# Later modulations by 64 rows and both column halves: a diffusion-transformer layer on one NeuronCore

## The chip, the cores and the metric

The kernel runs on one core of a Trainium2 chip. The metric is the device time of one execution in microseconds (us), the median over several runs. Lower is better. All arithmetic is float32; matrix products are made of float32 operands split into a high and a low part (`fp32r`), with three matmuls for each product.

## The reference, cut to what matters

The layer has nine modulation vectors for the latent tokens (from `c`) and nine for the context tokens (from `c_ctx`). Each is a row vector of 1024 times a 1024x1024 block of `w_mod`, plus a bias:

```
mod_lat = silu(c) @ w_mod[layer] + b_mod[layer]        # 9 * 1024 columns
mod_ctx = silu(c_ctx) @ w_mod[layer] + b_mod[layer]
ml = split(mod_lat, 9);  mc = split(mod_ctx, 9)
x  = x  + 0.5 * ml[2] * swiglu(modulate(rms_norm(x),  ml[0], ml[1]), ffn1_w_in, ffn1_w_out)
cx = cx + 0.5 * mc[2] * swiglu(modulate(rms_norm(cx), mc[0], mc[1]), ffn1_w_in, ffn1_w_out)
# mixers (convolution and attention) of x and cx, modulated by m = 3, 4, gated by ml[5]
# second feed-forward of x, modulated by m = 6, 7, gated by ml[8]; final norm
```

There are 1024 latent tokens, 256 context tokens, 1024 channels, 8 query heads and 2 key heads of 128, and feed-forward layers of 2816.

## The kernel before

The program is one long sequence of stages: start-up (tokens are loaded and transposed, the first modulations made), the first feed-forward's inner products (22 iterations `j`, each of which is a Winograd-like set of products `self.product(i)` of 12 matmuls of 128x128 weights by 512 columns), its outer products, the mixers' inner products, the heads (`tokens2`), attention, the merge, and the second feed-forward. Work off the main line is written as Python generators, whose steps are run between pieces of the main line. A scheduler then orders every engine's queue; matmuls marked `pinned` keep their place in the program. Each engine runs its own queue in order. Loads and stores are issued by SP's queue, in order.

The weights of each product pass through three buffers: `raw` (loaded), a high part made by ScalarE (`act.copy`, a cast) and a low part made by VectorE (`tensor_sub`), both named `wl` or `wh` with four buffers each. VectorE also adds the products' results up from PSUM (`u`, `v`, `b`, `c`), from five banks of tag `s`. So VectorE works both ahead of the TensorE (the low parts) and behind it (the additions).

The later modulations are such side work. `later_mod(m, ...)` (line 272) makes modulation `m`, one half of 512 columns after the other. For each half it loads eight tiles `rawm` of 128 rows by 512 columns (with `by_four`, four tiles that hold two of them), multiplies each by a column of `silu_c` and adds it to an accumulator `macc` on VectorE (one accumulator for each stream, latent and context), with a `yield` after each tile. After four steps more (`WAIT`) the accumulator is split into `acch` and `accl`, after six more steps two matmuls with a column of ones (`ones_r`) sum it over the partitions into one row of PSUM (bank tag `t`), ScalarE copies the row out in another order (`mrow`), SP's queue moves it into columns (`mcol`), and VectorE adds the bias into `modl` or `modc`. A half has 8 + 4 + 6 + 1 = 19 steps, a modulation 38.

What runs the steps: in the first feed-forward `STEPS` gives the number of steps after each iteration `j` (0, then 7, 7, 7, then 6 each, 0 at 13, 11 each from 14 on), with two steps after each of 14 context blocks behind iteration 13 (the batch). These steps are, in this order, the context's half of m = 1, the context's m = 0, the context's norm (`normc`), and m = 2, 3, 4 for both streams. m = 5 runs 8 steps at a time in the mixers, m = 6 and 7 (`by_four`) 8 at a time in the heads, and m = 8 three at a time in the second feed-forward.

```
STEPS = (0, 7, 7, 7, 6, 6, 6, 6, 6, 6, 6, 6, 6, 0, 11)
BATCH = 2
WAIT = 4
tpool = ctx.enter_context(tc.tile_pool(name="tpool", bufs=11))      # ttile: rawm, macc, acch, accl, mrow and others
```

Of the kernel before, what the change touches and what calls it, by code (L numbers as in the profile page):

```python
# [18 lines left out]
P = 128  # L19
D = 1024  # L20
KD = D // P
# [22 lines left out]
WAIT = 4  # L44
# [7 lines left out]
def tile_dit_layer(  # L52
# [73 lines left out]
    def ps_t(n=512):  # L126
        return psum.tile([P, 512], F32, tag="t", name=uniq("pt"), bufs=2)[:, :n]
# [62 lines left out]
    silu_c = const.tile([P, 16], F32, name="silu_c")  # L190
    act.activation(out=silu_c[:], in_=cols[:, :16], func=AF.Silu)

    modl = const.tile([P, 72], F32, name="modl")
    modc = const.tile([P, 40], F32, name="modc")


    def split(src, hi, lo, lo_eng=None, hi_eng=None):

        if hi_eng is dve:
            dve.tensor_copy(out=hi, in_=src)  # L200
        else:
            act.copy(out=hi, in_=src)
        (lo_eng or dve).tensor_sub(out=lo, in0=src, in1=hi.bitcast(F32))
# [65 lines left out]
            transpose(pr[:, j * P : (j + 1) * P], y[:, j : j + 1].to_broadcast([P, P]), pinned=True)  # L269
        return pr  # L270

    def later_mod(m, halves=(0, 1), streams=None, by_four=False):

        if streams is None:
            streams = (0, 1) if m < 5 else (0,)
        for half in halves:
            raws = fetch_mod(m, half, False) if by_four else None
            accs = [ttile(f"macc{v}") for v in streams]
            o = m * D + half * 512
            for k in range(KD):  # L280
                if by_four:
                    raw = raws[k // 2][:, k % 2]
                else:
                    raw = ttile("rawm")
                    load(out=raw, in_=w_mod[0, k * P : (k + 1) * P, o : o + 512])
                for acc, v in zip(accs, streams):
                    s = silu_c[:, v * 8 + k : v * 8 + k + 1]
                    if k == 0:
                        dve.tensor_scalar(out=acc, in0=raw, scalar1=s, scalar2=None, op0=ALU.mult)
                    else:  # L290
                        dve.scalar_tensor_tensor(out=acc, in0=raw, scalar=s, in1=acc, op0=ALU.mult, op1=ALU.add)
                yield
            for _ in range(WAIT):
                yield
            parts = []
            for acc in accs:
                ah, al = ttile("acch", dt=F32R), ttile("accl", dt=F32R)
                split(acc, ah, al)
                parts.append((ah, al))
            for _ in range(6):  # L300
                yield
            for (ah, al), v in zip(parts, streams):
                mod, pm = (modl, modc)[v], ps_t()
                matmul(pm[:1], ones_r[:], ah, start=True, stop=False, pinned=True)
                matmul(pm[:1], ones_r[:], al, start=False, stop=True, pinned=True)
                row = ttile("mrow")
                act.copy(
                    out=row[:1].rearrange("o (p j) -> o j p", j=4), in_=pm[:1].rearrange("o (j p) -> o j p", j=4)
                )
                mcol = small("mcol", 4)  # L310
                sp.dma_start(out=mcol[:], in_=row[:1])
                c0 = m * 8 + half * 4
                dve.tensor_add(out=mod[:, c0 : c0 + 4], in0=mcol[:], in1=bcol[:, c0 : c0 + 4])
            yield

    def fetch_mod(m, half, pinned=True):
        raws = []
        for kk in range(KD // 2):
            raw = atile("rawm", (P, 2, 512))
            o = m * D + half * 512  # L320
            load(raw[:], w_mod[0, kk * 256 : (kk + 1) * 256, o : o + 512].rearrange("(a p) n -> p a n", p=P), pinned)
            raws.append(raw)
        return raws
# [833 lines left out]
    hc = Context("h1ch", F32R), Context("h1cl", F32R)  # L1157
    normc = modulated_norm(xc, *hc, CC, gain1, mods, 0)

    def all_later_mods():  # L1160
        yield from later_mod(1, (1,), (1,))
        yield from later_mod(0, (0, 1), (1,))
        part_gain(gain1["c"], 0, "g1", "c", 0, 8)
        for _ in normc:
            yield
        for m in range(2, 5):
            yield from later_mod(m)
# [744 lines left out]
```

## Time and profile before

| | |
|---|---|
| runs | median 2631.92 us of 3 (2631.13 to 2632.04) |
| span of the profiled execution, first to last instruction | 2631.1 us (the runs' median is 0.8 us above it) |
| TensorE matmuls | busy 2609.9 us, 12665 instructions |
| TensorE weight loads | busy 2176.1 us |
| VectorE | busy 1997.4 us, 3360 instructions |
| ScalarE | busy 1183.5 us |
| GpSimd | busy 545.8 us |
| DMA | 384.69 MB, mean 146 GB/s |
| granted TensorE clock, mean | 0.998 |

"Busy" is the union of an engine's instructions; a matmul's record spans its passage through the pipeline, so consecutive matmuls overlap in the records. In the rows below, L90 is a helper through which every operation passes, so groups are told apart by the names of what they write and read. `x180` is a count. A tile's buffer number is left out in the profile (`ps` for every bank of that name).

### The profile page before, as it was taken

How to read it: one execution, taken by the hardware profiler on the slowest of the kernel's cores; microseconds unless marked ns; L12 is line 12 of the kernel's file. 1: busy time of each engine (PE TensorE's matmuls, PEld its weight loads, DVE VectorE, ACT ScalarE, POOL GpSimd, SP SyncE). 2: the span in 40 equal slices, each digit the busy share in tenths (PEclk: the TensorE clock that was granted, in tenths of full speed). 3: DMA queues.
4: the chain of work that ended last, by engine and by line, in shares of the span. 5: the costliest groups of instructions: out<-in, count | busy, mean ns of one | idle time of the engine just before them, and what ended most of it. 6: DMA issues, size and time to landing. Idle time of an engine off the chain costs nothing.

```text
span 2631.1 us, 35379 instructions
## 1 busy us (share of the span) xinstructions
PE 2609.9 (99%) x12665; PEld 2176.1 (83%) x12665; DVE 1997.4 (76%) x3360; ACT 1183.5 (45%) x2343; POOL 545.8 (21%) x425
## 2 busy tenths in 40 slices
PE   8999999999999999999999999999999999999998
PEld 5888899888888888888888888888888888888888
DVE  5888976877897879977788576676457886667996
ACT  6533454333454642333355566574237333334553
POOL 0133201221010034333022112132000442321100
PEclk9999999999999999999999999999999999999999
DMA  8665465345973365542522322113425653227831
GB/s 324 205 210 182 149 215 173 106 131 185 327 184 117 124 205 160 163 134 89 200 77 85 86 87 65 33 37 118 158 85 176 201 167 96 90 80 286 191 84 65
DMA packets 372905, 384.69 MB, mean 146 GB/s; under 512 B 19686, under 2 KB 256376, under 8 KB 372728
## 3 DMA queue, kind: packets, MB, share of 16 engines
q1 hardware_dynamic: 363288, 363.52, 42.1%
q0 software_dynamic: 9440, 18.91, 4.3%
q8 instruction: 99, 1.62, 0.2%
q14 instruction: 78, 0.64, 0.1%
HBM read 310.45 MB, written 71.86 MB: 145 GB/s over the span
## 4 chain that ended last, share of the span: by engine, by line
PE 94%; DVE 3%; DMA 1%; ACT 1%; issue 1%; SPq 0%; DVEq 0%; ACTq 0%
PE ps L90 81%; PE pt L90 8%; PE po L90 6%; DMA rawm<-in_w_mod_dram 1%; DVE xb L90 0%; DVE wl L90 0%; DVE macc L90 0%; DVE m L90 0%; DVE y L90 0%; DVE pts L90 0%; DMA xtok<-in_x_dram 0%; DVE x L90 0%; DVE r L90 0%; SPq L90 0%; DVE rs_t L90 0%
## 5 line engine op out<-in xcount | busy, mean ns | idle before, releaser
L90 PE MATMUL ps<-r,wl 128*128 128x512 f32 x5196 | 1198.3, 390 | 3.6 <-ACT r L90 1.3
L90 PEld LDWEIGHTS ps<-r,wl 128*128 128x128 f32 x5196 | 972.4, 188 | 207.7 <-ACT r L90 1.6
L90 ACT CAST wl<-sum 128x512 fp32r<-128x512 f32 x218 | 134.1, 622 | 294.4 <-PE ps L90 227.1
L90 ACT CAST wl<-raw 128x512 fp32r<-128x512 f32 x287 | 178.2, 622 | 193.1 <-PE ps L90 147.9
L90 DVE TENSOR_TENSOR wl<-raw,wl 128x512 fp32r<-128x512 f32 x287 | 210.2, 736 | 61.0 <-ACT wl L90 59.3
L90 DVE TENSOR_TENSOR wl<-sum,wl 128x512 fp32r<-128x512 f32 x218 | 196.9, 904 | 33.5 <-ACT wl L90 32.3
L90 POOL TENSOR_TENSOR sum<-raw 128x512 f32<-128x512 f32 x55 | 76.4, 1389 | 680.6 <-DMA raw<-in_ffn_w_in_dram 345.3
L90 DVE SCALAR_TENSOR_TENSOR macc<-rawm,silu_c,macc 128x512 f32<-128x512 f32 x178 | 145.4, 835 | 17.1 <-DMA rawm<-in_w_mod_dram 16.6
L90 DVE TENSOR_TENSOR u<-u,ps 128x512 f32<-128x512 f32 x186 | 126.5, 680 | 32.2 <-PE ps L90 32.1
L90 ACT CAST rh<-hid 128x512 fp32r<-128x512 f32 x132 | 82.2, 623 | 139.4 <-PE ps L90 112.3
L90 POOL TENSOR_TENSOR sum<-raw,sum 128x512 f32<-128x512 f32 x55 | 76.7, 1395 | 287.0 <-DVE wl L90 284.0
L90 DVE TENSOR_TENSOR pts<-pt,pts 128x512 fp32r<-128x512 f32 x160 | 107.3, 686 | 36.2 <-ACT pts L90 34.6
L90 DVE TENSOR_REDUCE m<-ps 128x1 f32<-128x256 f32 (+1 forms) x192 | 111.0, 597 | 29.4 <-PE ps L90 28.5
L90 ACT CAST pts<-pt 128x512 fp32r<-128x512 f32 x160 | 92.2, 597 | 85.5 <-PE pt L90 84.4
L90 PE MATMUL ps<-rh,wl 128*128 128x512 f32 x360 | 122.8, 390 | 0.0
L90 PE MATMUL ps<-wh,r 128*128 128x512 f32 x384 | 120.7, 392 | 0.0
L90 DVE TENSOR_TENSOR rl<-hid,rh 128x512 fp32r<-128x512 f32 x132 | 91.0, 693 | 29.9 <-ACT rh L90 19.4
L90 ACT CAST wh<-raw 128x512 fp32r<-128x512 f32 (+1 forms) x85 | 68.2, 803 | 95.5 <-PE ps L90 74.9
L90 PE MATMUL ps<-kl,qs 128*128 128x512 f32 x384 | 104.0, 394 | 0.1
L90 PE MATMUL ps<-rh,wh 128*128 128x512 f32 x300 | 102.8, 389 | 0.0
L90 PE MATMUL ps<-y,wc 128*128 128x512 f32 x384 | 95.3, 391 | 0.2 <-DVE g L90 0.2
L90 POOL TENSOR_TENSOR sum<-sum,raw 128x512 f32<-128x512 f32 x55 | 87.8, 1597 | 5.7 <-PE ps L90 3.9
(325 smaller groups left out, 5102.3 us busy)
## 6 DMA issues: line engine op xcount, KB each, us to landing
raw<-in_ffn_w_in_dram SPq DMA_DIRECT2D x131, 512.0 KB
raw<-in_ffn_w_out_dram SPq DMA_DIRECT2D x72, 512.0 KB
raw<-in_w_in_dram SPq DMA_DIRECT2D x64, 512.0 KB
rawm<-in_w_mod_dram SPq DMA_DIRECT2D x104, 256.0 KB
hid<-hd SPq DMA_DIRECT2D x40, 512.0 KB
ucd<-uc SPq DMA_DIRECT2D x33, 512.0 KB
rawm<-in_w_mod_dram SPq DMA_DIRECT2D x32, 512.0 KB
ws<-in_ffn_w_out_dram POOLq DMA_DIRECT2D x26, 512.0 KB, 6.4
```

Source lines behind the costliest of these rows:

```text
L90: inst = getattr(self.engine, name)(*args, **kw)
```

## The change

Each step now takes 64 rows of `w_mod` and all 1024 columns: the tile `rawm` holds columns 0 to 511 of the 64 rows in partitions 0 to 63, and columns 512 to 1023 of the same rows in partitions 64 to 127. One accumulator thus holds both halves. Two DMAs fill a tile, one for each half of the partitions. A step multiplies by a column of `silu_r`, which has the 64 values of `silu` in both halves of the partitions; four small DMAs make it from `silu_c` once (`spread_silu`). At the end one pair of matmuls with two one-hot columns (`halves_r`: ones in partitions 0 to 63, and in 64 to 127) sums the two halves into two rows of PSUM, one copy takes both out, two DMAs turn them into eight columns, and one addition adds the bias. A modulation has 16 + 4 + 6 + 1 = 27 steps. The context's half of m = 1 keeps the old form, under the name `later_half`.

```diff
+    one_hot = const.tile([P, 2], F32, name="one_hot")
+    pool.memset(one_hot[:], 0.0)
+    for h in range(2):
+        pool.memset(one_hot[h * 64 : (h + 1) * 64, h : h + 1], 1.0)
+    halves_r = const.tile([P, 2], F32R, name="halves_r")
+    act.copy(out=halves_r[:], in_=one_hot[:])
+    silu_r = const.tile([P, 32], F32, name="silu_r")
+
+    def spread_silu():
+        by = silu_r[:].rearrange("p (a s) -> p a s", s=2)
+        for h in range(2):
+            for i in range(2):
+                sp.dma_start(out=by[h * 64 : (h + 1) * 64, :, i], in_=silu_c[i * 64 : (i + 1) * 64, :])
...
-    def later_mod(m, halves=(0, 1), streams=None, by_four=False):
+    def later_mod(m, streams=None, by_four=False):
...
+        def rows(t, n):
+            return w_mod[0, t * 64 : (t + n) * 64, m * D : (m + 1) * D].rearrange("(a r) (h n) -> h r a n", r=64, h=2)
+        accs = [ttile(f"macc{v}") for v in streams]
+        for t in range(16):
+            if by_four and t % 8 == 0:
+                raws = []
+                for i in range(4):
+                    raw = atile("rawm", (P, 2, 512))
+                    for h in range(2):
+                        load(raw[h * 64 : (h + 1) * 64], rows(t + 2 * i, 2)[h])
+                    raws.append(raw)
+            if by_four:
+                raw = raws[t % 8 // 2][:, t % 2]
+            else:
+                raw = ttile("rawm")
+                for h in range(2):
+                    load(raw[h * 64 : (h + 1) * 64], rows(t, 1)[h, :, 0])
+            for acc, v in zip(accs, streams):
+                s = silu_r[:, v * 16 + t : v * 16 + t + 1]
...
+            yield
+        yield from mod_sums(accs, streams, m * 8, halves_r, 2)
...
+    def mod_sums(accs, streams, c0, sums, n):
+        for _ in range(WAIT):
+            yield
...
+        for (ah, al), v in zip(parts, streams):
+            mod, pm = (modl, modc)[v], ps_t()
+            matmul(pm[:n], sums[:], ah, start=True, stop=False, pinned=True)
+            matmul(pm[:n], sums[:], al, start=False, stop=True, pinned=True)
+            row = ttile("mrow")
+            act.copy(
+                out=row[:n].rearrange("o (p j) -> o j p", j=4), in_=pm[:n].rearrange("o (j p) -> o j p", j=4)
+            )
+            mcol = small("mcol", 8)
+            for h in range(n):
+                sp.dma_start(out=mcol[:, h * 4 : (h + 1) * 4], in_=row[h : h + 1])
+            dve.tensor_add(out=mod[:, c0 : c0 + 4 * n], in0=mcol[:, : 4 * n], in1=bcol[:, c0 : c0 + 4 * n])
+        yield
...
+    spread_silu()
     def all_later_mods():
-        yield from later_mod(1, (1,), (1,))
-        yield from later_mod(0, (0, 1), (1,))
+        yield from later_half(1, 1, (1,))
+        yield from later_mod(0, (1,))
```

The built programs show how this moves instructions. On the TensorE, behind iteration 6 of the first feed-forward (counted from 0), the program before has the sum of the first half of m = 0 (`pt` is the PSUM row, `ps` the products, `r` their moving operand, `wl` the low part of their weights):

```order
L90 MATMUL ps_2062<-r_155_777,wl_1995 128x512 x3
L90 MATMUL ps_2062<-r_178_875,wl_1995 128x512 x3
L90 MATMUL ps_2062<-r_205_993,wl_1995 128x512 x3
L90 MATMUL ps_2062<-r_224_1068,wl_1995 128x512 x3
L90 MATMUL pt_2079<-acch_1967,ones_r 1x512
L90 MATMUL pt_2079<-accl_1968,ones_r 1x512
L90 MATMUL ps_2100<-r_162_802,wl_2021 128x512 x3
L90 MATMUL ps_2100<-r_185_900,wl_2021 128x512 x3
L90 MATMUL ps_2100<-r_212_1018,wl_2021 128x512 x3
L90 MATMUL ps_2100<-r_227_1079,wl_2021 128x512 x3
```

The sum of the second half stands 62 rows further on, again as one pair with `ones_r`. The changed program has no sum at the first place, and one pair for both halves behind iteration 8, 11 rows ahead of where the second half's stood:

```order
L90 MATMUL ps_2329<-r_155_784,wl_2262 128x512 x3
L90 MATMUL ps_2329<-r_178_882,wl_2262 128x512 x3
L90 MATMUL ps_2329<-r_205_1000,wl_2262 128x512 x3
L90 MATMUL ps_2329<-r_224_1075,wl_2262 128x512 x3
L90 MATMUL pt_2346<-acch_2234,halves_r 2x512
L90 MATMUL pt_2346<-accl_2235,halves_r 2x512
L90 MATMUL ps_2406<-r_162_809,wl_2288 128x512 x3
L90 MATMUL ps_2406<-r_185_907,wl_2288 128x512 x3
L90 MATMUL ps_2406<-r_212_1025,wl_2288 128x512 x3
L90 MATMUL ps_2406<-r_227_1086,wl_2288 128x512 x3
```

Over the whole program the 46 matmuls of the later sums become 24: eleven pairs with `halves_r`, one pair with `ones_r`.

On VectorE, in iteration 12 ahead of its `b` (`u`, `v` and `b` are the iteration's additions, `nt` and `h1cl` belong to the context's norm, `wl` is a low part), the program before has no modulation work; it is still at the norm:

```order
L90 TENSOR_TENSOR nt_2709<-xc_97,pt_2706 128x256
L90 TENSOR_TENSOR nt_2714<-xc_97,pt_2706 128x256
L90 TENSOR_SCALAR nt_2709<-nt_2709,gain_c,modc 128x256
L90 TENSOR_TENSOR u_2598<-u_2598,ps_2724 128x512
L90 TENSOR_SCALAR nt_2714<-nt_2714,gain_c,modc 128x256
L90 TENSOR_TENSOR wl_2739<-sum_2644,wl_2739 128x512
L90 TENSOR_TENSOR h1cl_1262<-nt_2709,h1ch_1260 128x256
L90 TENSOR_TENSOR h1cl_1262<-nt_2714,h1ch_1260 128x256
L90 TENSOR_TENSOR v_2719<-u_2598,ps_2742 128x512
L90 TENSOR_TENSOR wl_2766<-raw_2756,wl_2766 128x512
L90 TENSOR_TENSOR b_2720<-v_2719,ps_2769 128x512
```

The changed program has reached m = 2 there, for both streams:

```order
L90 SCALAR_TENSOR_TENSOR macc_537_2765<-rawm_2776,silu_r,macc_537_2765 128x512
L90 TENSOR_TENSOR v_2791<-u_2651,ps_2814 128x512
L90 TENSOR_TENSOR u_2513<-u_2513,v_2655 128x512
L90 TENSOR_TENSOR wl_2838<-raw_2828,wl_2838 128x512
L90 SCALAR_TENSOR_TENSOR macc_536_2764<-rawm_2781,silu_r,macc_536_2764 128x512
L90 TENSOR_TENSOR wo_3229<-raw_3067,wo_3229 128x512
L90 TENSOR_TENSOR wl_2858<-raw_2828,wl_2858 128x512
L90 SCALAR_TENSOR_TENSOR macc_537_2765<-rawm_2781,silu_r,macc_537_2765 128x512
L90 TENSOR_TENSOR wl_2876<-s_552_2833,wl_2876 128x512
L90 SCALAR_TENSOR_TENSOR macc_536_2764<-rawm_2786,silu_r,macc_536_2764 128x512
L90 TENSOR_TENSOR b_2792<-v_2791,ps_2841 128x512
```

The whole chain of steps stands earlier, since a modulation is eleven steps shorter. In the program before, `b` of iterations 10, 11 and 12 (`b_2453`, `b_2603`, `b_2720`) stand at rows 328, 356 and 378 of VectorE's queue; in the changed one (`b_2518`, `b_2656`, `b_2792`) at 346, 380 and 409. The `b` of iterations 8 and 13 stand at rows 299 and 416 before, and at 299 and 438 after: between them the changed program has 19 multiply-adds into `macc`, two first multiplications and two low parts more, and one `accl` less. The next `b` (iteration 14) stands at 577 and 601.

On SP's queue, at the start, the program before has

```order
L90 DMA raw_654<-in_ffn_w_in_dram 128x4x128 x2
L90 DMA raw_720<-in_ffn_w_in_dram 128x4x128 x2
L90 DMA half_292<-in_ffn_w_in_dram 128x4x128 x2
L90 DMA rawm_295<-in_w_mod_dram 128x2x512
L90 DMA rawm_297<-in_w_mod_dram 128x2x512
L90 DMA rawm_299<-in_w_mod_dram 128x2x512
```

and the changed one has the first of the four DMAs of `spread_silu` ahead of the first product's weights (`half`); the other three stand later, among stores of `xd`:

```order
L90 DMA raw_661<-in_ffn_w_in_dram 128x4x128 x2
L90 DMA raw_727<-in_ffn_w_in_dram 128x4x128 x2
L90 DMA silu_r<-silu_c 64x16x1
L90 DMA half_299<-in_ffn_w_in_dram 128x4x128 x2
L90 DMA rawm_302<-in_w_mod_dram 128x2x512
L90 DMA rawm_304<-in_w_mod_dram 128x2x512
L90 DMA rawm_306<-in_w_mod_dram 128x2x512
```

SP's queue has 975 DMAs before and 1091 after: 136 loads of `rawm` become 248, and `silu_r` has four; the stores into `mcol` stay 23. VectorE has 22 instructions fewer (3360 and 3338): 11 `accl`, 11 additions of the bias; and 11 of the first multiplications become multiply-adds. ScalarE has 11 `acch` and 11 `mrow` fewer.

More of the change, by code (lines that the diff above doesn't have):

```diff
@@ L270, in bcast @@
         return pr
-    def later_mod(m, halves=(0, 1), streams=None, by_four=False):
+    def later_mod(m, streams=None, by_four=False):
         if streams is None:
             streams = (0, 1) if m < 5 else (0,)
[L276 to L282, printed above, removed]
-                else:
[L284 to L313, printed above, removed]
-            yield
@@ new lines, in rows @@
+        def rows(t, n):
[17 more added lines that the diff above has]
+                s = silu_r[:, v * 16 + t : v * 16 + t + 1]
+                if t == 0:
+                    dve.tensor_scalar(out=acc, in0=raw, scalar1=s, scalar2=None, op0=ALU.mult)
+                else:
+                    dve.scalar_tensor_tensor(out=acc, in0=raw, scalar=s, in1=acc, op0=ALU.mult, op1=ALU.add)
+            yield
@@ new lines, in later_mod, with later_half @@
+        yield from mod_sums(accs, streams, m * 8, halves_r, 2)
+    def later_half(m, half, streams):
+        accs = [ttile(f"macc{v}") for v in streams]
+        o = m * D + half * 512
+        for k in range(KD):
+            raw = ttile("rawm")
+            load(out=raw, in_=w_mod[0, k * P : (k + 1) * P, o : o + 512])
+            for acc, v in zip(accs, streams):
+                s = silu_c[:, v * 8 + k : v * 8 + k + 1]
+                if k == 0:
+                    dve.tensor_scalar(out=acc, in0=raw, scalar1=s, scalar2=None, op0=ALU.mult)
+                else:
+                    dve.scalar_tensor_tensor(out=acc, in0=raw, scalar=s, in1=acc, op0=ALU.mult, op1=ALU.add)
+            yield
+        yield from mod_sums(accs, streams, m * 8 + half * 4, ones_r, 1)
@@ new lines, in mod_sums @@
+    def mod_sums(accs, streams, c0, sums, n):
+        for _ in range(WAIT):
+            yield
+        parts = []
+        for acc in accs:
+            ah, al = ttile("acch", dt=F32R), ttile("accl", dt=F32R)
+            split(acc, ah, al)
+            parts.append((ah, al))
+        for _ in range(6):
+            yield
[11 more added lines that the diff above has]
+            dve.tensor_add(out=mod[:, c0 : c0 + 4 * n], in0=mcol[:, : 4 * n], in1=bcol[:, c0 : c0 + 4 * n])
+        yield
```

## The prediction

> **What bounds the kernel now.** I read the page's totals first, then the shares of the chain that ended last.
>
> ```profile
> span 2631.1 us, 35379 instructions
> PE 2609.9 (99%) x12665; PEld 2176.1 (83%) x12665; DVE 1997.4 (76%) x3360; ACT 1183.5 (45%) x2343; POOL 545.8 (21%) x425
> PE 94%; DVE 3%; DMA 1%; ACT 1%; issue 1%; SPq 0%; DVEq 0%; ACTq 0%
> ```
>
> TensorE is busy for 99% of the span and holds 94% of the chain. Work taken from TensorE itself is worth its full price; work taken from another engine is worth something only where TensorE waits for that engine. The chain in order of time shows how dense the stretch with the changed work is:
>
> ```profile
> 135.37 40.83 PE ps L90 x180
> 176.20 0.47 PE pt L90 x2
> 176.67 40.83 PE ps L90 x180
> ```
>
> 180 products of 128x512 take 40.83 us, 0.227 us each, and the two matmuls of a modulation's sum take 0.47 us between them, with nothing ahead or behind. The waits of TensorE agree:
>
> ```profile
> PE pt L90 <- DMA vraw<-in_norm_g_dram: 3.2, 1, 3.2
> PE pt L90 <- DVE pts L90: 1.7, 7, 0.4
> PE ps L90 <- DVE wl L90: 0.7, 2, 0.4
> ```
>
> The largest is at the start. For VectorE's low parts (`wl`) it waited 0.7 us in all, so before the change VectorE is in time nearly everywhere. Next I ask how near VectorE is to being late where the change puts more on it. From one `b` to the next, iterations 8 to 13 of the first feed-forward, and the whole stretch (columns: us, then busy us and count of PE, PEld, DVE, ACT, POOL, then clock, DMA share, GB/s):
>
> ```profile
> 243.84:256.30 12.46, 12.46 (x56) 10.32 (x56) 12.27 (x17) 4.26 (x8) 6.00 (x4) 1.00 0.54 170
> 256.30:268.41 12.11, 12.11 (x55) 9.77 (x54) 9.71 (x15) 5.30 (x10) 5.55 (x4) 1.00 0.55 173
> 268.41:284.56 16.15, 16.15 (x74) 13.40 (x73) 15.12 (x30) 6.61 (x16) 7.76 (x5) 1.00 0.43 132
> 284.56:296.95 12.39, 12.39 (x57) 10.24 (x56) 12.36 (x23) 4.09 (x8) 4.61 (x3) 1.00 0.40 127
> 296.95:315.88 18.93, 18.93 (x86) 15.66 (x85) 18.93 (x40) 9.78 (x20) 1.29 (x1) 1.00 0.43 139
> 315.88:330.00 14.12, 14.12 (x104) 13.46 (x103) 10.07 (x18) 6.28 (x11) 0.00 (x0) 1.00 0.68 202
> 243.84:315.88 72.04, 72.04 (x322) 59.39 (x322) 68.39 (x119) 30.03 (x58) 25.20 (x17) 1.00 0.46 147
> ```
>
> TensorE streams all through. VectorE is busy for 68.39 of 72.04 us; only 3.65 us are free. This decides the forecast. Only behind it, in the batch of context blocks, has VectorE room again (10.07 of 14.12).
>
> **The sums.** 46 matmuls with one column become 24 with one or two.
>
> ```profile
> L90 PE MATMUL pt<-acch,ones_r 128*1 128x512 f32 x23 | 9.1, 396 | 0.0
> L90 PE MATMUL pt<-accl,ones_r 128*1 128x512 f32 x23 | 9.1, 396 | 0.0
> ```
>
> The records' 396 ns are passage through the pipeline; what the path pays is the chain's 0.47 us for two, about 0.234 each. No row has a 2-column sum with 512 streamed columns beside products, but one column costs what 128 cost to 3%, so I take 0.234 for two as well. 22 fewer times 0.234 is **-5.15 us**. No idle time stands ahead of these groups (0.0), so all of it is on the path. Bounds: -10.8 (if the 24 that remain cost nothing, 46 x 0.234) and 0.
>
> **Removed work beside the path.** Eleven splits, eleven copies of the row and eleven additions go:
>
> ```profile
> L90 DVE TENSOR_TENSOR accl<-macc,acch 128x512 fp32r<-128x512 f32 x26 | 17.7, 686 | 2.2 <-ACT acch L90 2.0
> L90 ACT CAST acch<-macc 128x512 fp32r<-128x512 f32 x26 | 16.2, 622 | 34.2 <-DVE macc L90 32.7 <-DMA hid<-hd 1.5
> L90 ACT COPY mrow<-pt 1x512 f32<-1x512 f32 x23 | 24.2, 1079 | 16.9 <-PE pt L90 16.9
> ```
>
> That is 11 x 0.69 = 7.5 us of VectorE and 11 x (0.62 + 1.08) = 18.7 us of ScalarE, hidden under TensorE's stream: 0. Eleven first multiplications become multiply-adds, 11 x (0.835 - 0.510) = 3.6 us of VectorE, likewise beside the path except in the stretch costed next:
>
> ```profile
> L90 DVE SCALAR_TENSOR_TENSOR macc<-rawm,silu_c,macc 128x512 f32<-128x512 f32 x178 | 145.4, 835 | 17.1 <-DMA rawm<-in_w_mod_dram 16.6
> L90 DVE TENSOR_SCALAR macc<-rawm,silu_c 128x512 f32<-128x512 f32 x26 | 12.8, 510 | 8.4 <-DMA rawm<-in_w_mod_dram 8.4
> ```
>
> **The earlier steps.** A modulation has 27 steps for 38, the numbers of steps behind each iteration stay, so the context's norm and then m = 2, with two multiply-adds to a step, move into iterations 9 to 12. By the order, between `b` of iteration 8 and of 13 VectorE gets 19 multiply-adds and two first multiplications more and one `accl` less (the two more low parts stood directly behind before). Rows of that stretch (200 to 330 us, and the last of 243.84 to 315.88):
>
> ```profile
> L90 DVE SCALAR_TENSOR_TENSOR macc<-rawm,silu_c,macc 128x512 f32<-128x512 f32 x8 | 8.0, 999 | 0.0
> L90 DVE TENSOR_SCALAR macc<-rawm,silu_c 128x512 f32<-128x512 f32 x2 | 1.0, 488 | 5.4 <-DMA rawm<-in_w_mod_dram 5.4
> L90 DVE TENSOR_TENSOR u<-u,ps 128x512 f32<-128x512 f32 x26 | 17.6, 678 | 0.3 <-PE ps L90 0.3
> L90 DVE TENSOR_TENSOR u<-u,v 128x512 f32<-128x512 f32 x9 | 10.6, 1182 | 1.0 <-ACT u L90 0.8
> L90 DVE SCALAR_TENSOR_TENSOR macc<-rawm,silu_c,macc 128x512 f32<-128x512 f32 x1 | 0.7, 740 | 0.0
> ```
>
> At 0.74 us: 14.1 + 1.0 - 0.7 = 14.4 us more, and 3.65 are free, so VectorE ends this stretch 10.7 us late. At 0.999 it would be 19.0 + 1.0 - 0.7 - 3.65 = 15.6. I take 0.74, the row in the stretch itself. Queued behind these rows on VectorE are the low parts that TensorE needs next and the additions that free its banks, so lateness becomes a wait of TensorE once the lead is used up. How long is the lead? The five intervals have a mean of 14.41 us, the last has 18.93: VectorE fell 4.5 us behind its even pace without a loss on TensorE. So 4.5 us of lead are shown, and 10.7 - 4.5 = **+6.2 us** lost. Bounds: 0 (four low parts and five banks hold more than the shown lead) to 15.6 (no lead left).
>
> The row of the multiply-add that reads two tiles from SBUF lies at 740 or at 999 ns, while the addition that reads a bank (`u<-u,ps`) keeps 678, and `u<-u,v`, with two SBUF inputs, has 1182. The Trainium skill ("SBUF — State Buffer", section "SBUF: two separate sides") has a rule for this pattern: VectorE and GpSimd share a port pair under an exclusive lock, and an instruction of VectorE with two SBUF inputs is blocked for the whole of a GpSimd instruction that reads SBUF. The trace agrees in kind (678 against 999 and 1182). By that rule the added multiply-adds cost more than 0.74 here, and the sum would be 4.9 us higher; it is the second rival below.
>
> **The loads.** 112 more loads and four small ones go to SP's queue.
>
> ```profile
> L90 SPq DMA_DIRECT2D rawm<-in_w_mod_dram x136: 327/425/2227, 3.7 to 2167.4; - x136
> DVE macc L90 <- DMA rawm<-in_w_mod_dram: 25.0, 21, 4.0
> ```
>
> 116 x 0.425 = 49 us of queue time over 2631, cheap. Each tile now arrives in two pieces of 64 partitions. VectorE waited 25.0 us for such tiles; no row has a load of 64 partitions. Between 0 and the doubling of these waits with half of it reaching TensorE (+12.5) I take **0**: where VectorE is late its tiles have long landed, and elsewhere TensorE doesn't notice VectorE's wait, since that is so for the 25.0 us now.
>
> **The start.** `spread_silu` puts one small DMA ahead of the first product's weights, `half`:
>
> ```profile
> 22.12 1.50 SPq L90 DMA_DIRECT2D half<-in_ffn_w_in_dram  x2
> 27.98 0.61 ACT L90 CAST wl<-half 128x512 fp32r<-128x512 f32 x1
>   ACT wh L90: 1.4, 1
> q1 hardware_dynamic: 144, 0.00, 1.1%
> rinvd<-rinv POOLq DMA_DIRECT2D x16, 2.0 KB, 8.6
> rrow<-rinvd POOLq DMA_DIRECT2D x16, 256.0 KB, 4.0
> ```
>
> The third row lists what was waited for before `half` was used: a ScalarE step, not the DMA. The fourth is a 6 us window with `mcol` alone: 144 packets took 1.1% of 16 engines, 7.3 ns each. The small DMA has 64 x 16 four-byte values; as 1024 packets they cost 7.5 engine-us, 0.5 us over 16. Bounds 0 and 4.6 (8.6 - 4.0, by how much the 2 KB rows land later than the 256 KB ones); nearest in kind is `mcol`, so **+0.5**. The other three come later, ahead of m = 0, and cost 0.
>
> **The heads.** By the order, m = 6 and 7 put 13 and 12 multiply-adds into units 0 and 2, where 8 and 6 stood:
>
> ```profile
> 1266.00:1340.00 74.00, 74.00 (x335) 60.26 (x334) 56.61 (x149) 27.47 (x86) 8.34 (x16) 1.00 0.46 159
> ```
>
> 11 more x 0.74 = 8.1 us against 17.4 free: 0, with 8.1 as the other end.
>
> **Sum.** -5.15 + 6.2 + 0.5 = +1.55 on the span of 2631.1. The median of the runs stands 0.8 above that span: 2631.92 + 1.55 = **2633.5 us**. 0.2% (5.3 us, about what a measurement of this kernel can tell from no change) reaches from 2626.7 to 2637.2.
>
> **The rivals.** *The lead holds.* Low parts and banks cover all 10.7 us, and the batch, where VectorE has room, pays it back: -5.15 + 0.5, **2627.3**, and a little below if the small DMA is hidden too. For it speaks the 0.7 us of waiting for `wl` with VectorE at 95%; against it, that by the order 22 of the multiplications (some 16 us) stand between the `b` of iterations 11 and 13, where VectorE was full without any. *The port.* Multiply-adds at 0.999 while GpSimd works (25.20 of 72.04 us): 15.6 - 4.5 = 11.1 lost, **2638.4**, slower; it decides from a loss of 9.9 us (5.15 - 0.5 + 5.3), which is a price of 0.93 us for each of the 19. Against it: GpSimd's work doesn't grow, so only a part of the 21 can meet it. *Late tiles.* Two pieces load at half the rate of one; the waits of VectorE double and half reaches TensorE: 2633.5 + 12.5 = **2646**, slower, decided where VectorE is already full (iterations 9 to 12). For it: the waits of 25.0; against it, a DMA share of 0.46 there. The Trainium skill speaks for it ("SBUF — State Buffer", section "Can I just issue two DMAs to hit both halves?"): two transfers, one at partition 0 and one at 64, gained 6% over a single one. No trace of before has such a load. *The small DMA is slow*, 4.6 instead of 0.5: **2637.6**.
>
> **How the numbers follow.** Forecast 0.50, its own range 2629.5 to 2637.2 (a lead of 2.5 to 8.5 us, and small terms): within 0.2% but for 0.02. The lead holds 0.25: faster by over 0.2% in 0.11, else within. The port 0.13, late tiles 0.08, the small DMA 0.04: slower. Faster 0.11, same 0.62, slower 0.27. The range 2626.0 to 2639.5 leaves out the late tiles and the lowest part of the second case.
>
> **What would show it.** Right: 24 `pt` sums at the same pitch; TensorE idle between 255 and 330 us by about 6 us, ended by VectorE's `wl`; VectorE without idle time there; no loss in the heads. The wait for `wl` staying near 0.7 us would show the lead; `macc` near 1.0 us there, the port; waits for `rawm` far above 25.0 us with TensorE idle behind them, late tiles; `wl<-half` later than 27.98, the start. Wrong altogether: a 2-column sum that is dearer than 0.234, or a loss in a stretch that I set at 0.

## The result, and the profile after

The changed kernel takes 2661.5 us (median of 4 runs, 2657.4 to 2665.3), against 2632.0 us: a ratio of 1.0114, interval 1.0099 to 1.0128. It is 29.5 us slower, outside the forecast range (2626.0 to 2639.5). The profiled execution has a span of 2660.9 us. Its totals and its chain:

```profile
span 2660.9 us, 35456 instructions
PE 2617.9 (98%) x12643; PEld 2179.4 (82%) x12643; DVE 1974.4 (74%) x3338; ACT 1162.4 (44%) x2322; POOL 540.9 (20%) x428
PE 82%; DVE 8%; DMA 4%; issue 2%; ACT 2%; SPq 2%; POOL 1%; DVEq 0%; POOLq 0%; ACTq 0%
```

TensorE has 22 matmuls fewer and yet 8 us more busy time (its granted clock is lower in places, 0.993 in the mean against 0.998). Its share of the chain falls from 94% to 82%; DMA and SP's queue, 1% and 0% before, now hold 6% together. The waits of TensorE (total, times, longest), and one of VectorE:

```profile
PE ps L90 <- ACT wl L90: 10.9, 5, 4.9
PE ps L90 <- DVE wl L90: 7.8, 7, 3.3
PE pt L90 <- DMA vraw<-in_norm_g_dram: 3.2, 1, 3.2
```

```profile
DVE macc L90 <- DMA rawm<-in_w_mod_dram: 36.9, 24, 5.9
```

The wait for VectorE's low parts grew from 0.7 to 7.8 us. That is near the forecast 6.2, but by chance: only 1.6 us of it lie at 250 to 350 us, where I had put them, and the longest one, 3.3 us, lies at 426 us (below). The wait above it is new: TensorE waits 10.9 us for casts of ScalarE, an engine that is busy 44% of the time. Such a cast is late because what it reads is late. Stretches of the changed kernel, in the columns used before (us, then busy us and count of PE, PEld, DVE, ACT, POOL, then clock, DMA share, GB/s):

```profile
200.00:250.00 50.00, 45.05 (x191) 36.75 (x190) 37.21 (x52) 13.74 (x25) 22.07 (x15) 0.93 0.66 203
250.00:350.00 100.00, 97.72 (x485) 81.42 (x484) 95.84 (x164) 39.84 (x77) 25.62 (x17) 1.00 0.56 172
350.00:460.00 110.00, 105.90 (x719) 98.30 (x718) 75.00 (x127) 52.08 (x97) 4.82 (x4) 0.98 0.74 203
1100.00:1150.00 50.00, 47.48 (x201) 38.29 (x200) 44.59 (x69) 14.47 (x27) 18.27 (x12) 0.97 0.51 158
2040.00:2200.00 160.00, 154.04 (x665) 124.87 (x664) 114.34 (x162) 53.52 (x95) 57.90 (x43) 0.99 0.58 178
```

TensorE idles in all five stretches, not in one; before, none of them had more than 0.1 us free on TensorE. The largest single pause, followed back along the chain:

```profile
196.29 3.11 DMA rawm<-in_w_mod_dram
...
200.30 6.76 DMA raw<-in_ffn_w_in_dram
207.06 0.07 issue
207.13 3.71 POOL sum L90 x3
210.84 0.02 issue
210.86 0.63 ACT wl L90
211.49 0.04 issue
211.53 3.78 PE ps L90 x8
```

It is a load of the feed-forward's weights (`raw`), issued at 200.30, on which GpSimd's sums, ScalarE's cast and TensorE wait in turn. Ahead of it on SP's queue stands a run of `rawm`. SP's queue in the kernel before:

```profile
172.31 0.38 SPq L90 DMA_DIRECT2D raw<-in_ffn_w_in_dram  x1
...
181.79 4.31 SPq L90 DMA_DIRECT2D rawm<-in_w_mod_dram  x4
188.34 0.38 SPq L90 DMA_DIRECT2D raw<-in_ffn_w_in_dram  x1
...
189.87 1.65 SPq L90 DMA_DIRECT2D rawm<-in_w_mod_dram  x2
...
192.62 0.38 SPq L90 DMA_DIRECT2D raw<-in_ffn_w_in_dram  x1
```

and in the changed one:

```profile
174.94 0.38 SPq L90 DMA_DIRECT2D raw<-in_ffn_w_in_dram  x1
...
185.44 2.39 SPq L90 DMA_DIRECT2D rawm<-in_w_mod_dram  x4
...
192.02 6.14 SPq L90 DMA_DIRECT2D rawm<-in_w_mod_dram  x8
...
200.30 1.49 SPq L90 DMA_DIRECT2D raw<-in_ffn_w_in_dram  x2
```

The changed kernel is 2.6 us behind here already (172.31 and 174.94, the same load). The next two loads of weights are issued at 188.34 and 192.62 before. In the changed kernel both stand behind the run, at 200.30 and just after, so they come some 9 and 6 us later still. Eight pieces of `rawm` took SP 6.14 us to issue. The queue's own row for all of them (shortest, median, longest ns of issuing one):

```profile
L90 SPq DMA_DIRECT2D rawm<-in_w_mod_dram x248: 368/594/4422, 3.7 to 2156.5; - x124
```

By these medians one piece of 128 KB holds SP's queue for 594 ns, and a whole tile of 256 KB held it for 425: a tile costs the queue 1.19 us, not 0.43. In the runs shown both are dearer and nearer to each other: 1.54 us for two pieces (6.14 / 4) against 1.08 for a whole tile (4.31 / 4). Weights that stand behind such a run come later by these differences, and here also by the pieces of the earlier steps that now stand ahead of them.

There is a second way to TensorE, through VectorE, which also runs its queue in order. The second-longest pause begins at 426 us. VectorE waits for pieces of `rawm` there, and a low part that TensorE needs stands behind the multiply-adds:

```profile
421.88 1.42 DVE L90 SCALAR_TENSOR_TENSOR macc<-rawm,silu_r,macc 128x512 f32<-128x512 f32 x2 [4.21 <-DMA rawm<-in_w_mod_dram]
...
425.17 1.42 DVE L90 SCALAR_TENSOR_TENSOR macc<-rawm,silu_r,macc 128x512 f32<-128x512 f32 x2 [1.28 <-DMA rawm<-in_w_mod_dram]
...
429.03 1.28 DVE L90 TENSOR_TENSOR wl<-raw,wl 128x512 fp32r<-128x512 f32 x2
```

```profile
429.77 0.50 PE L90 MATMUL ps<-h1ch,wl 128*128 128x256 f32 x2 [3.32 <-DVE wl L90]
```

The start, which I had set at 0.5 us: SP's queue, ScalarE's first cast of the weights, and the five microseconds behind it:

```profile
22.30 0.78 SPq L90 DMA_DIRECT2D silu_r<-silu_c  x1
23.13 4.17 SPq L90 DMA_DIRECT2D half<-in_ffn_w_in_dram  x2
```

```profile
29.31 0.62 ACT L90 CAST wl<-half 128x512 fp32r<-128x512 f32 x1 [1.21 <-DMA half<-in_ffn_w_in_dram]
```

```profile
30.00:35.00 5.00, 2.92 (x9) 2.43 (x10) 5.00 (x9) 3.21 (x6) 0.00 (x0) 0.64 0.96 319
```

Issuing `half` took 4.17 us behind the small load against 1.50, the first cast came 1.3 us later, and TensorE's granted clock was 0.64 in the five microseconds that follow, where it had been 1.00. That the clock is the change's doing isn't shown: e8 below has the start of the kernel before, and 0.50 there.

In the texts below, TensorE's loss in a stretch is the sum of what the starts of successive matmuls are further apart than usual for their kind (227 ns for 128x512; 235 for the late sums, and 429 for the start's own float32 matmuls of two columns). By it the whole program loses 87.2 us after and 52.4 before: 34.8 more, less 5.1 for 22 matmuls, is 29.7, against the 29.8 by which the spans differ. (The expectation of e2 speaks of 14.2 and 10.1 us at the start; there the start's matmuls were measured by the pitch of the late sums. By their own pitch it is 11.4 and 8.5.)

### The profile page after: what moved, and what is told of

The parts are those of the page before. It is cut to its first block, busy times and chain, and to the rows that moved or that the text cites. A ratio compares the mean times of both kernels' runs of the same rounds, so it can differ in the third digit from the quotient of the medians.

```text
span 2660.9 us, 35456 instructions
## 1 busy us (share of the span) xinstructions
PE 2617.9 (98%) x12643; PEld 2179.4 (82%) x12643; DVE 1974.4 (74%) x3338; ACT 1162.4 (44%) x2322; POOL 540.9 (20%) x428
## 4 chain that ended last, share of the span: by engine, by line
PE 82%; DVE 8%; DMA 4%; issue 2%; ACT 2%; SPq 2%; POOL 1%; DVEq 0%; POOLq 0%; ACTq 0%
PE ps L90 69%; PE pt L90 7%; PE po L90 6%; SPq L90 2%; DMA rawm<-in_w_mod_dram 1%; POOL sum L90 1%; DMA raw<-in_ffn_w_in_dram 1%; DVE wl L90 1%; DVE macc L90 1%; DVE u L90 1%; DVE y L90 1%; DVE nt L90 1%; ACT wl L90 0%; DVE xb L90 0%; ACT r L90 0%
## 5 line engine op out<-in xcount | busy, mean ns | idle before, releaser
L90 PE MATMUL ps<-r,wl 128*128 128x512 f32 x5196 | 1207.3, 392 | 19.9 <-ACT wl L90 10.9
L90 PEld LDWEIGHTS ps<-r,wl 128*128 128x128 f32 x5196 | 975.4, 189 | 229.7 <-ACT wl L90 13.2
L90 DVE TENSOR_TENSOR wl<-raw,wl 128x512 fp32r<-128x512 f32 x287 | 203.9, 715 | 71.9 <-ACT wl L90 70.8
L90 DVE TENSOR_TENSOR wl<-sum,wl 128x512 fp32r<-128x512 f32 x218 | 184.7, 850 | 59.2 <-ACT wl L90 58.1
L90 DVE SCALAR_TENSOR_TENSOR macc<-rawm,silu_r,macc 128x512 f32<-128x512 f32 x165 | 129.5, 803 | 33.1 <-DMA rawm<-in_w_mod_dram 32.8
L90 DVE TENSOR_TENSOR pts<-pt,pts 128x512 fp32r<-128x512 f32 x160 | 107.1, 684 | 36.4 <-ACT pts L90 34.8
L90 PE MATMUL ps<-h1ch,wl 128*128 128x256 f32 x448 | 84.0, 287 | 4.2 <-DVE wl L90 4.1
```

What stands on the lines that cost most here:

```text
L90: inst = getattr(self.engine, name)(*args, **kw)
```

## The experiments

Three theories. *The queue*: two loads to a tile hold SP's queue and delay the weights. *VectorE*: the earlier steps overload it in iterations 9 to 12, my forecast. *The start*: the small load delays `half`. Medians of the kernel before, run along with them, were 2631.3 to 2632.6 us.

**e1: one load to a tile, halves outermost.**

```diff
-                for h in range(2):
-                    load(raw[h * 64 : (h + 1) * 64], rows(t, 1)[h, :, 0])
+                load(raw, rows(t, 1)[:, :, 0])        # source (2, 64, 512)
```

> The changed kernel (2661.5 us), but each 64-row tile is filled by one load over all 128 partitions where there were two of 64 partitions (128 loads and 136 tiles' worth of bytes less nothing: the bytes stay). The queue theory (two loads to a tile keep SP's queue busy and stand in runs ahead of the weights; the losses at 200 to 250, 400 to 500 and 2100 to 2200 us, 24 us together, come from that): 2633 to 2640, with the start's 4 us and the stretch at 300 to 350 us (4 us) still there. VectorE's overload in iterations 9 to 12 as the cause: still above 2652. The start as the cause: still above 2655.

Measured: 3087.5 us, ratio 1.173 (1.171 to 1.175). It is above 2655 us, as two of the three theories said, but by 430 us that none of them explains, so it tells none of them apart. While such loads run alone the trace has

```profile
190.00:200.00 10.00, 7.31 (x32) 5.72 (x31) 4.50 (x7) 2.18 (x4) 1.30 (x1) 1.00 0.14 51
```

51 GB/s at a DMA share of 0.14, about two of 16 engines. The Trainium skill explains it ("DMA: Bandwidth & Descriptors", section "Rules for kernel authors"): an outermost dimension of size c below 16 confines a DMA to at most c engines. The source's outer dimension is 2. The trace agrees (2/16 = 0.125; in its packet records 2 to 4 packets are in flight at any time of this window).

**e2: the small loads late.** The four loads of `silu_r` keep their place in the program (`load(..., True)`).

> The changed kernel, but the four small loads that make silu_r are kept at their place in the program, behind the start, so that none stands ahead of the first product's weights on SP. The start theory: TensorE's loss in the first 50 us goes back from 14.2 to 10.1 us, so 4 us less than the changed kernel, about 2657; the queue theory agrees and says that the other 25 us stay. The rival that the small loads cost nothing: 2661, no difference.

Measured: 2659.1 us, ratio 1.0107 (1.0092 to 1.0122); 2.4 us below the changed kernel, which its interval does not separate from nothing. TensorE's loss in the first 50 us went from 11.4 to 8.8. The remaining 27 us stay: the start is at most a small part.

**e3: eleven empty steps at the end of a modulation**, so that it has 38 again.

```diff
         yield from mod_sums(accs, streams, m * 8, halves_r, 2)
+        for _ in range(11):
+            yield
```

> The changed kernel with eleven empty steps more at the end of each later modulation, so that it has 38 steps again and the work of the later ones stands where it stood before (only the loads, their number and the sums are the change's). VectorE's overload by the earlier steps as the cause: down by 15 us or more, to 2645 or less. The queue theory: still 2650 to 2662, with about 4 us less at 300 to 350 us.

Measured: 2661.8 us, ratio 1.0117 (1.0102 to 1.0132), no difference. VectorE's overload itself is real and goes: from the `b` of iteration 8 to that of 13 VectorE needs 85.2 us in the changed kernel, 71.7 in e3, 72.0 before. But the time doesn't follow, so it is not what makes the changed kernel slow. TensorE loses 0.7 us less at 250 to 350 us and 7.4 more at 350 to 400. It is not refuted as a smaller term: with weights late anyway, a VectorE that is late as well may cost little more.

**e4: the kernel before, its tiles loaded in two parts of 64 partitions.**

```diff
-                    load(out=raw, in_=w_mod[0, k * P : (k + 1) * P, o : o + 512])
+                    for h in range(2):
+                        load(out=raw[h * 64 : (h + 1) * 64], in_=w_mod[0, k * P + h * 64 : k * P + (h + 1) * 64, o : o + 512])
```

> The kernel before (2632.0 us) with one edit: each 128-row tile of the later modulations m = 0 to 5 and 8 is loaded in two loads of 64 partitions and 512 columns (104 loads become 208); steps, sums and VectorE's work as before. The queue theory: 2645 to 2658. VectorE's overload or the start as the cause: 2632, within 2 us.

Measured: 2654.8 us, ratio 1.0082 (1.0066 to 1.0099). The loads alone, with the old steps and sums, cost 23.5 us. The order on SP's queue is hardly another: of the 325 loads of weights named `raw`, six have more tiles ahead of them than in the kernel before.

**e5: one load to a tile, rows outermost.** Row r lies in partitions 2r and 2r+1.

```diff
-  .rearrange("(a r) (h n) -> h r a n", r=64, h=2)      ...  two loads of 64 partitions
+  .rearrange("(a r) (h n) -> r h a n", r=64, h=2)      ...  load(raw, rows(t, 1)[:, :, 0])
-                sp.dma_start(out=by[h * 64 : (h + 1) * 64, :, i], in_=silu_c[i * 64 : (i + 1) * 64, :])
+                sp.dma_start(out=by[h::2, :, i], in_=silu_c[i * 64 : (i + 1) * 64, :])
```

> The changed kernel, but row r of a tile lies in the partitions 2r (columns 0 to 511) and 2r+1 (columns 512 to 1023), so that one load fills all 128 partitions with the 64 rows as the outer dimension; the one-hot columns pick even and odd partitions, and silu_r is spread to match. Steps, sums and tiles as in the changed kernel. The queue theory (it is two loads of 64 partitions to a tile that cost the time): 2630 to 2640, with the start's loss and the 4 us at 300 to 350 us left. The rival that the one-load experiment went slow for another reason than its outer dimension of two: above 2700. VectorE's overload as the cause: 2655 to 2660.

Measured: 2642.1 us, ratio 1.0037 (1.0023 to 1.0050). 19.3 us of the 29.5 go with the second load; the time is 2 us above the range that I gave. While four such tiles are issued the DMA engines run full (317 GB/s for all transfers of the window; 0.87 of its 1.27 MB are in packets of 2 KB, the size that these loads have):

```profile
196.00:200.00 4.00, 4.00 (x19) 3.30 (x18) 2.82 (x3) 0.63 (x1) 3.96 (x3) 1.00 1.00 317
```

**e6: e5 with the small loads late**, as in e2.

> The kernel of e5 with the four small loads of silu_r kept behind the start. The queue theory with the start: 2626 to 2634, below e5 by 2 to 4 us, and at the lower end faster than before by the 5.15 us of the sums. The rival that the earlier steps cost their 4 to 6 us anyway: 2631 to 2636.

Measured: 2641.3 us, ratio 1.0033 (1.0021 to 1.0044): 0.8 us less, within the intervals, and above both expectations. What is left, some 9 us, is not the start.

**e7: the kernel before, its tiles loaded in two parts of 256 columns.**

```diff
-                    load(out=raw, in_=w_mod[0, k * P : (k + 1) * P, o : o + 512])
+                    for h in range(2):
+                        load(out=raw[:, h * 256 : (h + 1) * 256], in_=w_mod[0, k * P : (k + 1) * P, o + h * 256 : o + (h + 1) * 256])
```

> The kernel before (2631.3 us), with each 128-row tile of m = 0 to 5 and 8 loaded in two loads of 128 partitions and 256 columns (104 loads become 208, the bytes stay). If the number of loads on SP's queue is the cause: 2645 to 2660, as for two loads of 64 partitions (2654.8). If 64 partitions to a load are the cause: 2631 to 2637.

Measured: 2637.0 us, ratio 1.0018 (1.0009 to 1.0028): 4.9 us, at the edge of the second expectation and far from the first. The number of loads and the bytes are those of e4. The queue's rows of e4 and then of e7:

```profile
L90 SPq DMA_DIRECT2D rawm<-in_w_mod_dram x240: 367/588/2619, 3.7 to 2197.5; - x120
```

```profile
L90 SPq DMA_DIRECT2D rawm<-in_w_mod_dram x240: 327/430/3150, 3.7 to 2177.5; - x120
```

A part of 64 partitions holds the queue for 588 ns, one of 128 partitions for 430: 1.18 us and 0.86 us to a tile against 0.43. So it is not the count alone. What differs with the cost is the queue's time. The DMA engines, while runs of such parts are issued, first e4, then e7, then the kernel before with whole tiles:

```profile
189.00:194.00 5.00, 5.00 (x24) 4.14 (x23) 4.03 (x7) 1.76 (x3) 0.00 (x0) 1.00 0.57 166
```

```profile
189.00:193.00 4.00, 4.00 (x19) 3.33 (x18) 2.65 (x5) 0.62 (x1) 0.00 (x0) 1.00 0.60 164
```

```profile
182.00:186.00 4.00, 4.00 (x19) 3.34 (x18) 1.80 (x6) 0.62 (x1) 0.00 (x0) 1.00 0.93 282
```

Both kernels with parts leave the engines idle some 40% of the time. By the share, e4 moves 166 / 0.57 = 291 GB/s, before 282 / 0.93 = 303: the bytes of a 64-partition load are not markedly slower; the queue does not issue them fast enough. The packet records of these two windows agree. A packet of 2 KB takes 84 ns (median) in both; in e4 between 0 and 19 packets are in flight, before 13 to 19. So it isn't that half of the partitions keeps half of the engines busy: the engines fill up and run dry.

The cost doesn't follow the queue's time in proportion, though. In all, the parts hold the queue 78 us longer than whole tiles do in e4 and 54 us in e7, and cost 23.5 and 4.9 us. That the delay acts through the queue is read from the chains; no run issues these loads from another engine's queue, which would test it by itself.

**e8: the kernel before without the second matmul of each sum.**

```diff
-                matmul(pm[:1], ones_r[:], ah, start=True, stop=False, pinned=True)
-                matmul(pm[:1], ones_r[:], al, start=False, stop=True, pinned=True)
+                matmul(pm[:1], ones_r[:], ah, start=True, stop=True, pinned=True)
```

> The kernel before without the second matmul of each later sum (23 matmuls of one column; the low parts of the sums are left out, so the last digits differ). By the price of 0.234 us each, wholly on the path: 5.4 us less than before, 2626. If such a matmul is hidden or the time is given back elsewhere: within 1 us of before.

Measured: 2630.2 us, ratio 0.9993 (0.9983 to 1.0002): 1.9 us less. That is neither the 5.4 of the first expectation nor the 1 us or less of the second, and not surely anything. Its profile loses 3.6 us more than that of before: 2.3 at 650 to 700 us, 1.4 in the first 50 us, where the clock was

```profile
30.00:35.00 5.00, 4.45 (x13) 3.46 (x14) 5.00 (x9) 3.10 (x5) 0.00 (x0) 0.50 1.09 349
```

though this start has the same instructions as that of before (1.00 there).

**e9: e6 with eleven empty steps**, as in e3.

> The kernel of e6 (one load to a tile, the small loads late; 2641.3 us) with eleven empty steps more at the end of each later modulation, so that in iterations 11 and 12 VectorE has no multiply-adds again and the context's norm stands where it stood before. VectorE's overload by the earlier steps as the cause of what is left: TensorE's losses of 5.3 us at 250 to 350 and 2.5 us at 400 to 450 us go, 2633 to 2635. If what is left comes from the loads (64 rows in pieces of another order, twice as many tiles' rows for one modulation at a time): 2639 to 2642.

Measured: 2636.0 us, ratio 1.0014 (1.0005 to 1.0024): 5.3 us below e6, between the two expectations. The `b` of iterations 8 and 13 in e6, and then in e9:

```profile
245.32 0.68 DVE L90 TENSOR_TENSOR b<-v,ps 128x512 f32<-128x512 f32 x1
...
329.80 0.68 DVE L90 TENSOR_TENSOR b<-v,ps 128x512 f32<-128x512 f32 x1
```

```profile
245.66 0.68 DVE L90 TENSOR_TENSOR b<-v,ps 128x512 f32<-128x512 f32 x1
...
317.90 0.67 DVE L90 TENSOR_TENSOR b<-v,ps 128x512 f32<-128x512 f32 x1
```

With the earlier steps VectorE needs 84.5 us for this stretch, without them 72.2 (72.0 before): 12.2 us late. TensorE and VectorE at 250 to 350 us, e6 and then e9:

```profile
250.00:350.00 100.00, 96.88 (x491) 81.28 (x490) 96.37 (x163) 37.51 (x73) 23.69 (x16) 1.00 0.59 186
```

```profile
250.00:350.00 100.00, 100.00 (x531) 86.53 (x530) 86.04 (x150) 43.08 (x82) 23.95 (x16) 1.00 0.54 165
```

TensorE's loss at 250 to 350 us is 5.3 us in e6 and 0.3 in e9. This is VectorE's overload, once the late weights no longer cover it.

**e10: e6 with fewer steps behind each iteration.** `STEPS = (0, 7, 7, 7, 5, ..., 5, 0, 7)`.

> The kernel of e6 with fewer steps behind each iteration (five for six in iterations 4 to 12, seven for eleven from 14 on), which are enough for the 27 steps of a modulation; no multiply-adds stand in iterations 9 to 12, and fewer in 14 to 16. VectorE's overload as the cause: 2631 to 2634, at or below e9, since the later iterations are eased too. The rival that the loads cost it: 2639 to 2642.

Measured: 2639.2 us, ratio 1.0024 (1.0014 to 1.0034), by the medians 2.1 us below e6 and 3.2 above e9, neither clear of the intervals. It lies in the rival's range and outside that of VectorE's overload: my expectation failed. TensorE's loss at 250 to 350 us is 2.5 us, half of e6's; but 3.5 us stand at 200 to 250 and 4.0 at 350 to 400. In the latter TensorE pauses at 358 us behind a wait of VectorE for a tile (3.9 us), as at 426 us in the changed kernel; the cause of the former stays open.

**e11: e6 with the eleven steps in the middle of a modulation**, behind the eighth tile.

```diff
             yield
+            if t == 7:
+                for _ in range(11):
+                    yield
```

> The kernel of e6 (one load to a tile, the small loads late) with the eleven empty steps in the middle of a modulation, behind its eighth tile, so that each multiplication and each load stands at the step where the kernel before has it; only the sums are fewer (24 for 46) and the rows come in another order. If the rest of e9's time (2636.0) is the bunching of sixteen loads in a row: TensorE's losses of 2.7 us at 200 to 250 and 2.4 us at 350 to 400 us go, 2629 to 2633, and below before (2632.2) if no more than half of the 5.15 us of the sums is lost at the start. If one load with 64 outer rows costs the time by itself: 2635 to 2637.

Measured: 2631.5 us, ratio 0.9996 (0.9987 to 1.0005): 9.8 us below e6, 4.6 below e9, and equal to before by its interval. The intervals of e9 and e11 touch at 1.0005. The loss of 2.7 us at 200 to 250 us is gone; the one of e9 at 350 to 450 (3.3) stays, as 4.2, so one of the two losses that I named went and not the other. The profiled run of e11 is the longest of its eleven (2634.6 us) and that of e9 the shortest of its ten (2635.1), so the two profiles show no gain between them.

**e12: e11 with two loads of 64 partitions to a tile.**

> The same as e11 but with the changed kernel's two loads of 64 partitions to a tile; between the two kernels only the form of the loads differs, and no multiply-add stands in iterations 9 to 12. The queue theory: 2645 to 2655, 15 to 22 us above e11, as between e4 and before. VectorE's overload as the cause of the changed kernel's time: within 3 us of e11.

Measured: 2650.9 us, ratio 1.0071 (1.0057 to 1.0085): 19.4 us above e11. This is the form of the loads by itself, with every step where it was before. The order of the queue hardly differs: of the 325 loads of `raw`, 15 have more tiles ahead of them than in the kernel before in e11, and 17 in e12. (In the changed kernel and in e6 it is 95, in e9 69.)

## Why the prediction was wrong

**The step that failed is "The loads".** It multiplied 116 loads by 0.425 us, called 49 us of queue time over 2631 "cheap", and took 0, with +12.5 as the other end. It cost 19.4 us (e12 less e11), 23.5 by itself in the kernel before (e4). Four things were wrong in it. The price: a piece of 64 partitions holds the queue for 594 ns, 40% longer than the whole tile of before. The average: the queue's time was spread over the whole span, but the loads come in runs, and the weights stand behind the run in the same in-order queue. The weights: I asked who waits for `rawm`, and did not ask who waits for what is queued behind it, although the order of SP's queue, read further than the start, shows the runs (two loads of `raw` now stand behind twelve pieces where one stood behind four tiles). And VectorE: I said that TensorE doesn't notice VectorE's wait for tiles, since it didn't before. At 426 us it does (3.3 us), because low parts stand behind the waiting multiply-adds. How the 19.4 us divide between these two ways isn't told apart; VectorE's wait for tiles grew by 11.9 us in the changed kernel (25.0 to 36.9), and is 37.5 in e12 against 22.6 in e11.

**The rival "late tiles"** named the loads as the cause, but not how or where. It is not half the rate (291 and 303 GB/s for a full share), but the time to issue. The waits of VectorE grew by half and didn't double. And the losses aren't where VectorE is full: e12 loses 7.9 us at 200 to 250 us and 8.1 at 350 to 400, but 2.1 at 250 to 350. The Trainium skill ("SBUF — State Buffer", section "Can I just issue two DMAs to hit both halves?") says that two transfers to the two halves "measured at only +6% over a single one"; as a warning this agrees with e12, but in e4's window it is the issuing that falls short, and not the rate of the engines.

**The earlier steps** (+6.2) were right in mechanism and place, and near in size. VectorE was 13.2 us late in the changed kernel (85.2 us for 72.0) and 12.2 in e6, where I had 10.7. TensorE lost 4.2 us at 250 to 350 us in the changed kernel and 5.3 in e6, and e9 got 5.3 us of time back. That the loss comes near 6.2 is in part luck: VectorE was later than I said, and the lead was longer, some 7 us in e6 (12.2 less the 5.0 that e9 takes from the loss) where I had 4.5. In the changed kernel itself the late weights hide the term (e3). The multiply-adds there took 824 ns in the mean, between my 740 and the 999 of the rival "the port", and short of the 930 from which that rival decides. I set the same steps at 0 elsewhere; the next item has those.

**The heads and other places** (0): the heads themselves cost nothing. At 1100 to 1150 us, in the mixers, m = 5 cost TensorE 2.5 us (50.00 busy before, 47.48 after, 50.00 again in e11), and at 2040 to 2200 us, with m = 8, 6 us; I had not priced m = 5 and m = 8 at all. e11, with the empty steps in the middle, is 4.6 us below e9, so sixteen steps in succession cost something even in the good form; whether by their loads or their multiplications isn't shown. Fewer loads of weights stand behind tiles in e11 (15 against 69), which speaks for the loads.

**The start** (+0.5, bounds 0 to 4.6): `half` came 1.3 us later, TensorE's loss in the first 50 us rose by 2.9, and e2 got 2.6 of it back. I counted the small load's bytes; what it did was to hold the queue (4.17 us to issue two loads against 1.50) and so to lengthen a pause of TensorE. Half of the 2.9 may be the clock's chance: e8, with the start of the kernel before, lost 1.4 us more there than that kernel. As a difference of run times the term is not resolved.

**The sums** (-5.15): the price holds in the trace. Rows of the changed kernel:

```profile
254.42 0.40 PE L90 MATMUL pt<-acch,halves_r 128*2 128x512 f32 x1
254.66 0.40 PE L90 MATMUL pt<-accl,halves_r 128*2 128x512 f32 x1
```

0.24 us apart, so a second column costs nothing. As a gain in time it was never seen whole: 1.9 us in e8 (interval from a gain of 4.5 to a loss of 0.5), 1.1 in e11 (from a gain of 3.4 to a loss of 1.3). The two profiles give back 3.6 and 6.4 us in small losses elsewhere, in part at the start, where the clock differs from run to run. Whether 5 us can be had by fewer sums stays open.

Put together, by medians: 19.4 for the loads (e12 less e11), 9.8 for the steps' places (e6 less e11), 2.4 for the start (e2) and -1.1 for all the rest (e11 less before) come to 30.5, against 29.5 measured; the terms need not add exactly, since one wait can cover another (e3). With two loads to a tile the steps' places cost 8.2 (e2 less e12), and by that way the sum is 28.9. e11, the best version found, beats the changed kernel by 30 us and before by nothing that can be told.

## What to carry to other kernels

Price a load twice: by the time that it holds its queue, from the queue's own row, and by what stands behind it in that in-order queue; a load that is not urgent itself can delay one that everybody needs. The same goes for the engine that uses it: an instruction that waits for a late tile holds up those behind it. Splitting a load in two to suit a layout is not free even at the same bytes; look for a layout that one load can fill, with a dimension of many rows outermost. And when side work is shortened, it does not vanish from where it was but arrives earlier somewhere else: keep it at the steps where it was hidden, and only then count the gain.

## What the runs showed of the hardware

- A load of 64 partitions by 2 KB held SP's queue longer (588 to 594 ns median) than one of 128 partitions by 2 KB (425) or by 1 KB (430). The one load of e5 and e11, with 64 rows outermost, lay between (552 and 558). Why is open.
- Loads whose source has an outer dimension of 2 ran alone at 51 GB/s (e1); with 64 outermost (e5) the engines ran full, 317 GB/s with what else they moved.
- A long pause of TensorE is followed by a lower granted clock, so that it costs more than its idle time. In the changed kernel the clock is 0.50 behind the pauses of 5.3, 3.6 and 3.3 us at 206, 426 and 2126 us, and 1.00 behind those of 1.7 us at 311 and 2.3 us at 2160. In between it goes either way (1.00 behind 3.0 us at 204 us in e3, 0.50 behind 2.7 us at 249 us in e12), and two pauses close together, of 1.7 and 1.5 us at 1134 and 1136 us, had 0.51 behind them. Behind the pause at 206 us:

```profile
208.00:212.50 4.50, 0.97 (x2) 0.83 (x3) 2.55 (x4) 1.64 (x4) 2.83 (x3) 0.60 0.79 251
```

TensorE's loss at 200 to 250 us is 7.2 us, of which 5.0 were idle (45.05 of 50.00 busy). At the start, the clock at 30 to 35 us was 1.00, 0.64, 0.50 and 0.51 in four profiles (before, after, e8, e11), and TensorE's loss in the first 50 us 8.5, 11.4, 9.9 and 10.1.
